# Pace of the projection, four held half tiles, and ordered turns in a hybrid attention layer on one core

## The chip, the core and the metric

The kernel runs on one core of a Trainium2 chip. The core has five engines that run their own instruction queues in order: TensorE (PE in the profile, with its weight loads as PEld), VectorE (DVE), ScalarE (ACT), GpSimd (POOL) and SyncE (SP, which issues the DMAs here). The metric is device microseconds of one launch. The time before is the median of three runs, 1719.52 us (1718.66 to 1720.41).

## What is computed

One layer of a streaming encoder over 1024 prompt tokens, and over 8 x 16 new tokens with caches of 1024 past frames. Everything is float32.

```python
h = rmsnorm(x, g_mix)
q_a, k_a, v_a, q_b, k_b, v_b = split_heads(h, w_in)      # group A: 8 heads x 64, group B: 8 heads x 64
a = stick_breaking(q_a, k_a, v_a)                        # causal over the full past, no softmax
o_b = chunk_band_prompt(q_b, k_b, v_b, rel_table)        # own chunk of 64 and the 8 before, with a bias
a, o_b = per_head_rmsnorm(a), per_head_rmsnorm(o_b)
x = x + concat(a, o_b) @ w_out
h = rmsnorm(x, g_ffn)
x = x + (silu(h @ w_gate) * (h @ w_up)) @ w_down
x = x + sigmoid(rmsnorm(x, g_ple) @ w_ple_gate) * (p @ w_ple_proj)
y = rmsnorm(x, g_final)
```

Stick-breaking: with z the scaled scores, the weight of key k for query q is sigmoid(z) times the product of sigmoid(-z) over the keys between them. The new tokens do the same against their caches, and the new keys and values are outputs too.

## The kernel before

**Number format and tiles.** Each float32 operand of a large product is split into a high part (a cast on ACT, L159) and a low part (a subtraction, `sub`, L105, on POOL or DVE), and `mm3` (L99 to L102) issues three matmuls for each product. Tokens come in nine tiles of 128: 0 to 7 are the prompt, 8 holds the new tokens.

**Order of the work.** Python generators yield after a step, and `advance(main, side, ratio)` (L733) runs `ratio` steps of `side` for each step of `main`. This gives the program order. Outside the blocks that order an engine by hand, a planner then walks the program with a model of the engines' times: on each engine it issues the earliest instruction in program order that its model holds to be ready, so a later instruction can be pulled ahead of an earlier one that still waits. The order that comes out is fixed, and each engine's queue then keeps it on the chip. `tc.issue_after(ins)` ties the instructions of its block that run on the engine of `ins` behind `ins`; those on other engines stay free. The tie is an order and no semaphore.

**Stages around the change.**

- The q/k/v projection (`qkv`, L227) yields 96 steps. Its last 30 (`others` for the values of group B, `queries` of group B) run beside the attention: `advance(project, att, 1.95)` at L818.
- The attention (`attention`, L515) goes through eight pairs of heads, 0 to 3 of group A and 4 to 7 of group B, and through 8 query tiles of each head: 128 units. A step does `scores` of unit i (S, L579 and L580), `flip` of unit i-5 (transposes of the weights, L610, a cast on ACT, L614, and a subtraction on DVE), and `outputs` of two units at a time (`po`, L633 and L634). In group A, `scores` has two sigmoids on ACT (L582, L583), the running product as two scans on DVE (L111 over the tile's own 128 keys, L114 over the keys before) and a product on POOL (L592); in group B, a bias and a minimum on DVE (L586) and an exponential on ACT (L594). When both heads of a pair are done, `turn` (transposes L648, reductions L649 and L654) and `finish` (power and products on POOL, L121 and L671) write the pair's normed output to DRAM (`mixp`); the last pair stays in SBUF (`osb`).
- When the projection has ended, its pools are closed and the decode of group B (`decode`, L334) begins, with `embed` (L827), in the same places. Three attention steps go before and 40 beside them (L875, L877).
- Then the output projection's upper half (`half_out`, L925): the heads of pairs 0 to 3 are loaded (`fetch_mix`, L888, tile `mixn`, four buffers), turned (`turn_mix`, L901: three transposes on PE, L904, a scaled copy on ACT, L907, a subtraction on DVE, L908) and multiplied with the upper 512 rows of `w_out`: 18 half tiles, one for each token tile and each half of the 1024 columns, 12 matmuls of 512 columns each. x is added on DVE (L937) and the sum goes to DRAM (`resid`). One of these steps goes beside each attention step (L947), then come the turns of pairs 4 to 6 and, after the attention, of pair 7 (L950).
- `w_b` (L952) are the lower 512 rows of `w_out`. Weights have one raw buffer and two pairs of places for their parts; L952 takes the places of the two halves before it in turn.
- The next stage (from L1096) adds the lower half for each token tile (`lower`, L996, tile `ps`), in the order 0, 4, 1, 5, 2, 6, 8, 3, 7, with the second column half two tiles behind the first, and goes on to the norm and the feed-forward part.

PSUM has two banks for turns and half tiles (tag M), which both use.

Of the kernel before, what the change touches and what calls it, by code (L numbers as in the profile page):

```python
# [13 lines left out]
F32 = mybir.dt.float32  # L14
# [3 lines left out]
ALU = mybir.AluOpType  # L18
# [4 lines left out]
P = 128  # L23
# [3 lines left out]
NT = 9  # L27
# [5 lines left out]
SKEW = 2  # L33
R2 = 1.2
LAG, RAWS, PT = 5, 7, 2
VLAG, AHEAD = (2, 1), 2


@with_exitstack
def tile_hymba_step(  # L40
# [37 lines left out]
    nc = tc.nc  # L78
    V, A, G, T = nc.vector, nc.scalar, nc.gpsimd, nc.tensor
# [4 lines left out]
    ident = cst.tile([P, P], F32, name="ident")  # L84
# [7 lines left out]
    x_tok = [x_prompt[0, t * P : (t + 1) * P, :] for t in range(NP)] + [x_sample.rearrange("b i d -> (b i) d")]  # L92
# [6 lines left out]
    def mm3(out, ah, al, bh, bl, start, stop):  # L99
        T.matmul(out, lhsT=ah, rhs=bh, start=start, stop=False)  # L100
        T.matmul(out, lhsT=ah, rhs=bl, start=False, stop=False)  # L101
        T.matmul(out, lhsT=al, rhs=bh, start=False, stop=stop)  # L102
# [113 lines left out]
    resid = dram.tile([NT * P, D], F32, name="resid")  # L216
# [293 lines left out]
            yield  # L510


    kept = []

    def attention(ap_, ps, lag):  # L515
        def prepare(p8):
# [80 lines left out]
        def flip(st, hh, t, w):  # L597
            grp = st["grp"]
            g = t // 2
            kb0 = max(0, t - 4) if grp else 0  # L600
            base = max(0, 2 * g - 4) if grp else 0
            if t % 2 == 0:
                st["wt"] = [ap_.tile([P, 6 + g % 2 * 2, 256], F32R, name=f"wt{n}", tag=f"wta{n}{g % 2}") for n in "hl"]
            wth, wtl = st["wt"]
            nb = t + 1 - kb0
            for c0 in range(0, nb, 4):
                c1 = min(c0 + 4, nb)
                pt = ps["t"].tile([P, 512], F32, name="pt", tag="T")
                for c in range(c0, c1):
                    T.transpose(pt[:, (c - c0) * P : (c - c0 + 1) * P], w[:, c * P : (c + 1) * P], ident)  # L610
                pv = pt[:, : (c1 - c0) * P].rearrange("p (k n) -> p k n", n=P)
                ks = slice(kb0 + c0 - base, kb0 + c1 - base)
                qs = slice((t % 2) * P, (t % 2) * P + P)
                A.copy(wth[:, ks, qs], pv)  # L614
                sub(V, wtl[:, ks, qs], pv, wth[:, ks, qs])
            return st["wt"]

        def outputs(st, hh, g, wt):
            wth, wtl = wt
            grp = st["grp"]  # L620
            base = max(0, 2 * g - 4) if grp else 0
            nkb = 2 * g + 2 - base
            po = ps["t"].tile([P, 512], F32, name="po", tag="T")
            order = [2 * g] + [kb for kb in range(base, 2 * g + 2) if kb != 2 * g]
            for i, kb in enumerate(order):
                c0, c1 = 0, 256
                if kb == 2 * g + 1:
                    c0 = P
                if grp and kb == 2 * g - 4:
                    c1 = P  # L630
                vs = st[hh]["v"][:, kb].rearrange("p a d -> p (a d)")
                dst = po[:, c0:c1]
                T.matmul(dst, lhsT=vs, rhs=wth[:, kb - base, c0:c1], start=(i == 0), stop=False)  # L633
                T.matmul(dst, lhsT=vs, rhs=wtl[:, kb - base, c0:c1], start=False, stop=(i == nkb - 1))  # L634
            if g == 0:
                st["ob"] = ap_.tile([P, D], F32, name="ob", tag="ob", bufs=1)
            A.copy(st["ob"][:, g * 256 : g * 256 + 256], po[:, :256])
# [81 lines left out]
    ps = {}  # L719
# [13 lines left out]
    def advance(main, side, ratio, steps=None):  # L733

        due, n = 0.0, 0
        while steps is None or n < steps:
            if next(main, "end") == "end":
                break
            n += 1
            due += ratio  # L740
            while due >= 1.0:
                due -= 1.0
                next(side, None)
        return n

    ch = Chunks(pool(ctx, "w1", "left"), "w", 2048, 1, 2)
    hp = pool(right, "h1", "right")
    stg = pool(right, "stg", "right", 2)
    first, start = ExitStack(), ExitStack()
    banks(right, "right", o=2)  # L750
    banks(start, "left", t=4, g=1)
    hT = Transposed()
# [4 lines left out]
    with tc.tile_pool(name="x1", bufs=2, side="right") as xp, tc.manual_schedule(engines=all_engines):  # L757

        xs = []
# [26 lines left out]
        project = qkv(ch, hT, stg, w_first, ch.raw(cols(w_in[0], 3), KT, 256))  # L786
# [28 lines left out]
    at = pool(left, "at", "left")  # L815
    run, pairs, done = attention(at, ps, LAG)
    att = run(range(8))
    advance(project, att, 1.95)  # L818
    right.close()


# [37 lines left out]
    def chain(*parts):  # L859
        for p_ in parts:  # L860
            yield from p_
# [19 lines left out]
    hT = Transposed()  # L881
# [3 lines left out]
    mp = pool(dstack, "mp", "right", 2)  # L885
# [15 lines left out]
    def turn_mix(k, g, srcs):  # L901
        pt = ps["m"].tile([P, 384], F32, name="pt", tag="M")
        for o, src in enumerate(srcs):
            T.transpose(pt[:, o * P : (o + 1) * P], src, ident)  # L904
        h, l = hT.rows(g, k)
        gk = g_out[:, k : k + 1]
        A.activation(h, pt, AF.Copy, scale=gk)  # L907
        V.scalar_tensor_tensor(l, pt, gk, h.bitcast(F32), op0=ALU.mult, op1=ALU.subtract)  # L908

    def mix(ks):  # L910

        got = []
        for k in ks:
            while k not in done:
                yield
            for g in range(3):
                got.append((k, g, fetch_mix(k, g)))
                if len(got) > 2:
                    turn_mix(*got.pop(0))
                yield  # L920
        for x in got:
            turn_mix(*x)
            yield

    def half_out():  # L925

        yield from mix(range(4))
        for c in range(2):
            wh, wl = out_weights(0, c)
            for t in range(NT):  # L930
                cs = slice(c * 512, (c + 1) * 512)
                xs = mp.tile([P, 512], F32, name="xs", tag="xs", bufs=3)
                nc.sync.dma_start(xs, x_tok[t][:, cs])
                acc = ps["m"].tile([P, 512], F32, name="acc", tag="M")
                for k in range(4):
                    mm3(acc, *hT.tok(t, k), wh[:, k], wl[:, k], k == 0, k == 3)
                V.tensor_tensor(xs, xs, acc, op=ALU.add)  # L937
                nc.sync.dma_start(resid[t * P : (t + 1) * P, cs], xs)
                yield

    def out_weights(grp, c):

        return ch.load(w_out[0, grp * 512 : grp * 512 + 512, c * 512 : (c + 1) * 512].rearrange("(k p) c -> p k c", p=P),
                       4, 512)

    side = chain(half_out(), mix(range(4, 7)))
    advance(att, side, 1.0)  # L947
    for _ in side:
        pass
    for _ in mix([7]):  # L950
        pass
    w_b = [out_weights(1, c) for c in range(2)]  # L952
    left.close()
    dstack.close()
    hstack[0].close()
# [135 lines left out]
    marks = []  # L1091

    A.activation(xg.tile([P, 1], F32, name="any", tag="r_n"), nhalf[:, 0:1], AF.Sigmoid)
    order = [0, 4, 1, 5, 2, 6, 8, 3, 7]
    xs, first_half, rows = {}, {}, []
    fetch(order[0], 0)  # L1096
    with ExitStack() as planned:
        for i in range(NT + SKEW):
# [14 lines left out]
            if j == NT - 2:  # L1113
                w = gate_up_parts(raw, V)
# [15 lines left out]
    with tc.tile_pool(name="ph4b", bufs=2, side="right", reuse_waits="tile") as p4b:  # L1130
# [12 lines left out]
        for i in range(n_chunk):  # L1143
# [25 lines left out]
            c = bank()  # L1169
# [546 lines left out]
```

## Time and profile before

| | us |
|---|---|
| median of three timed runs | 1719.52 |
| the profiled execution, in all | 1712.64 |
| its span, first to last instruction | 1710.6 |

The profile is of that one execution. A row of a stage gives its stretch, its length, the busy time of each engine with the number of instructions, the mean granted TensorE clock (1.00 is full speed), the busy share of the DMA engines and the data rate. A row of a group names line, engine and operation, what is written from what, the count, then the busy time and the mean ns of one, and the idle time before them with what ended it. A row of a wait names who waited for whom, with the sum in us, the number of times and the longest. A row of the timeline starts with the start in us and the duration; in brackets is the idle time of the engine before it. Matmuls overlap in the pipeline, so their rows' durations add to more than the time that they take; the distance from start to start is what one costs in a row of them.

### The profile page before, as it was taken

How to read it: one execution, taken by the hardware profiler on the slowest of the kernel's cores; microseconds unless marked ns; L12 is line 12 of the kernel's file. 1: busy time of each engine (PE TensorE's matmuls, PEld its weight loads, DVE VectorE, ACT ScalarE, POOL GpSimd, SP SyncE). 2: the span in 40 equal slices, each digit the busy share in tenths (PEclk: the TensorE clock that was granted, in tenths of full speed). 3: DMA queues.
4: the chain of work that ended last, by engine and by line, in shares of the span. 5: the costliest groups of instructions: out<-in, count | busy, mean ns of one | idle time of the engine just before them, and what ended most of it. 6: DMA issues, size and time to landing. Idle time of an engine off the chain costs nothing.

```text
span 1710.6 us, 27738 instructions
## 1 busy us (share of the span) xinstructions
PE 1651.7 (97%) x10308; PEld 1421.3 (83%) x10308; DVE 1099.0 (64%) x1716; ACT 807.1 (47%) x1713; POOL 805.7 (47%) x652
## 2 busy tenths in 40 slices
PE   8999999989997999898989999999999999999998
PEld 7999888989996887787868888888888878878887
DVE  6111444379889666854787666666565597798875
ACT  5323545366778777643543233333332244433673
POOL 2313301277356411322345555555555379968763
PEclk9999999999998999999999999999999999999999
DMA  5847888665369885854422222222222597722222
GB/s 193 276 151 219 275 292 293 187 187 168 116 181 277 276 266 163 252 176 169 153 82 96 96 96 95 96 93 87 86 89 95 214 367 256 257 79 111 99 98 99
DMA packets 172810, 293.49 MB, mean 172 GB/s; under 512 B 16642, under 2 KB 96258, under 8 KB 170371
## 3 DMA queue, kind: packets, MB, share of 16 engines
q1 hardware_dynamic: 172674, 291.71, 52.0%
q8 instruction: 82, 1.34, 0.3%
q14 instruction: 54, 0.43, 0.1%
HBM read 204.77 MB, written 86.90 MB: 171 GB/s over the span
## 4 chain that ended last, share of the span: by engine, by line
PE 78%; DVE 7%; DMA 6%; ACT 3%; POOL 3%; issue 2%; SPq 1%; POOLq 0%; DVEq 0%; ACTq 0%
PE ps L1058 24%; PE ps L100 6%; PE ps L101 6%; PE ps L102 6%; PE pt L1321 4%; PE pt L1058 3%; PE ps L1321 3%; PE pt L610 2%; PE pt L405 2%; PE acc L468 2%; DMA v<-sv 2%; DVE keep L114 2%; PE po L634 1%; PE sdec L427 1%; PE S L579 1%
## 5 line engine op out<-in xcount | busy, mean ns | idle before, releaser
L105 POOL TENSOR_TENSOR wlo<-wraw,whi 128x512 fp32r<-128x512 f32 (+1 forms) x119 | 211.3, 1798 | 139.7 <-ACT whi L159 138.5
L100 PE MATMUL ps<-whi,hTh 128*128 128x256 f32 x576 | 167.7, 291 | 1.3 <-ACT st L267 1.3
L101 PE MATMUL ps<-wlo,hTh 128*128 128x256 f32 x576 | 164.2, 285 | 0.0
L102 PE MATMUL ps<-whi,hTl 128*128 128x256 f32 x576 | 163.7, 284 | 0.1
L159 ACT CAST whi<-wraw 128x512 fp32r<-128x512 f32 (+1 forms) x122 | 88.6, 744 | 71.4 <-PE ps L1058 28.6
L100 PEld LDWEIGHTS ps<-whi,hTh 128*128 128x128 f32 x576 | 110.4, 192 | 7.9 <-issue 5.7
L592 POOL TENSOR_TENSOR w<-w,keep 128x127 f32<-128x127 f32 (+4 forms) x64 | 78.6, 1230 | 74.8 <-DVE keep L114 64.5
L102 PEld LDWEIGHTS ps<-whi,hTl 128*128 128x128 f32 x576 | 110.4, 192 | 0.8 <-DVE hTl L105 0.4
L101 PEld LDWEIGHTS ps<-wlo,hTh 128*128 128x128 f32 x576 | 110.5, 192 | 0.2
L614 ACT CAST wth<-pt 128x512 fp32r<-128x512 f32 (+1 forms) x192 | 84.4, 466 | 44.5 <-PE pt L610 43.9
L105 DVE TENSOR_TENSOR wtl<-pt,wth 128x512 fp32r<-128x512 f32 (+1 forms) x192 | 94.1, 513 | 14.8 <-ACT wth L614 14.7
L114 DVE TENSOR_TENSOR_SCAN keep<-keep,zero 128x128 f32<-128x128 f32 (+7 forms) x64 | 101.6, 1588 | 1.7
L610 PE MATMUL pt<-ident,w 128*128 128x128 f32 x528 | 90.4, 284 | 8.5 <-DVE wtl L105 4.4
L610 PEld LDWEIGHTS pt<-ident,w 128*128 128x128 f32 x528 | 64.2, 144 | 21.6 <-DVE wtl L105 6.0
L579 PE MATMUL S<-qk 128*128 128x384 f32 (+2 forms) x192 | 71.9, 376 | 6.5 <-ACT keep L583 4.4
L633 PE MATMUL po<-wth,vk 128*128 128x256 f32 (+1 forms) x304 | 76.5, 283 | 1.5 <-DVE wtl L105 1.2
L105 POOL TENSOR_TENSOR actl<-actr,acth 128x1024 fp32r<-128x1024 f32 (+1 forms) x22 | 61.2, 2782 | 34.2 <-DMA sr<-acts 20.7
L634 PE MATMUL po<-wtl,vk 128*128 128x256 f32 (+1 forms) x304 | 73.4, 285 | 0.0
L406 DVE COPY kT<-pt 128x512 f32<-128x512 f32 x48 | 33.0, 687 | 53.4 <-PE pt L405 49.5
L101 PE MATMUL ps<-hTl,whi 128*128 128x384 f32 x192 | 65.4, 341 | 0.0
L102 PE MATMUL ps<-hTh,wlo 128*128 128x384 f32 x192 | 65.3, 340 | 0.0
L100 PE MATMUL ps<-hTh,whi 128*128 128x384 f32 x192 | 65.3, 340 | 0.0
(441 smaller groups left out, 5292.1 us busy)
## 6 DMA issues: line engine op xcount, KB each, us to landing
draw<-in_cache_sb_k SPq DMA_DIRECT2D x32, 512.0 KB, 5.7
draw<-in_cache_sb_v SPq DMA_DIRECT2D x32, 512.0 KB, 5.7
act<-sg SPq DMA_DIRECT2D x11, 1152.0 KB
actr<-act SPq DMA_DIRECT2D x22, 576.0 KB, 9.5
wraw<-in_w_in SPq DMA_DIRECT2D x11, 1024.0 KB, 8.7
wraw<-in_w_gate SPq DMA_DIRECT2D x11, 1024.0 KB, 5.5
wraw<-in_w_up SPq DMA_DIRECT2D x11, 1024.0 KB, 5.4
v<-sv SPq DMA_DIRECT2D x36, 256.0 KB, 4.7
```

Of the source, the lines that this page charges most:

```text
L100: T.matmul(out, lhsT=ah, rhs=bh, start=start, stop=False)
L101: T.matmul(out, lhsT=ah, rhs=bl, start=False, stop=False)
L102: T.matmul(out, lhsT=al, rhs=bh, start=False, stop=stop)
L105: return eng.tensor_tensor(out, a, hi.bitcast(F32), op=ALU.subtract)
L114: V.tensor_tensor_scan(rev, rev, zero[:, 0:1].to_broadcast([P, n - d]), keep[:, n - d : n - d + 1], op0=ALU.mult, op1=ALU.max)
L159: A.copy(h[:, o], v[:, o])
L579: T.matmul(sc, lhsT=hd["qq"][:, qs], rhs=hd["kkh"][:, kc], start=True, stop=False)
L610: T.transpose(pt[:, (c - c0) * P : (c - c0 + 1) * P], w[:, c * P : (c + 1) * P], ident)
L614: A.copy(wth[:, ks, qs], pv)
L634: T.matmul(dst, lhsT=vs, rhs=wtl[:, kb - base, c0:c1], start=False, stop=(i == nkb - 1))
L1058: T.matmul(out, lhsT=a[x][:, k], rhs=b[y][:, k], start=(not more and k == 0 and n == 0), stop=(k == 3 and n == 2), skip_group_check=more)
L1321: T.matmul(out, lhsT=a[i][:, x, m * P : (m + 1) * P], rhs=b[j][:, x], start=(not more and x == 0 and n == 0), stop=(x == 1 and n == 2), sk ...
```

## The change

The pace of the attention beside the projection goes from 1.95 to 2.13 steps. `flipped` keeps the last transpose or output matmul that the attention has traced, and all turns of pairs 0 to 6 that run beside or right behind the attention are tied behind it on PE. The half tiles take the order of the next stage; the last four of the second column half (token tiles 6, 8, 3, 7) are taken out of the steps beside the attention and traced after the turns of pairs 4 to 6, tied behind the attention's last output matmul. The second of the two lower weight halves gets its low part from DVE instead of POOL.

```diff
+HELD = 4
+ORDER = [0, 4, 1, 5, 2, 6, 8, 3, 7]
...
-    kept = []
+    kept, flipped = [], []
...
-                    T.transpose(pt[:, (c - c0) * P : (c - c0 + 1) * P], w[:, c * P : (c + 1) * P], ident)
+                    flipped[:] = [T.transpose(pt[:, (c - c0) * P : (c - c0 + 1) * P], w[:, c * P : (c + 1) * P], ident)]
...
-                T.matmul(dst, lhsT=vs, rhs=wtl[:, kb - base, c0:c1], start=False, stop=(i == nkb - 1))
+                flipped[:] = [T.matmul(dst, lhsT=vs, rhs=wtl[:, kb - base, c0:c1], start=False, stop=(i == nkb - 1))]
...
-    advance(project, att, 1.95)
+    advance(project, att, 2.13)
...
                 if len(got) > 2:
-                    turn_mix(*got.pop(0))
+                    with tc.issue_after(flipped[0].ins):
+                        turn_mix(*got.pop(0))
                 yield
         for x in got:
-            turn_mix(*x)
+            with tc.issue_after(flipped[0].ins):
+                turn_mix(*x)
             yield
+
+    def half_tile(t, c, wh, wl):
+        cs = slice(c * 512, (c + 1) * 512)
+        xs = mp.tile([P, 512], F32, name="xs", tag="xs", bufs=3)
+        nc.sync.dma_start(xs, x_tok[t][:, cs])
+        acc = ps["m"].tile([P, 512], F32, name="acc", tag="M")
+        for k in range(4):
+            mm3(acc, *hT.tok(t, k), wh[:, k], wl[:, k], k == 0, k == 3)
+        V.tensor_tensor(xs, xs, acc, op=ALU.add)
+        nc.sync.dma_start(resid[t * P : (t + 1) * P, cs], xs)
 
     def half_out():
 
         yield from mix(range(4))
         for c in range(2):
             wh, wl = out_weights(0, c)
-            for t in range(NT):
...
+            for t in ORDER if c == 0 else ORDER[:-HELD]:
+                half_tile(t, c, wh, wl)
                 yield
+        held.append((wh, wl))
...
+    def out_weights(grp, c, eng=None):
+
+        src = w_out[0, grp * 512 : grp * 512 + 512, c * 512 : (c + 1) * 512].rearrange("(k p) c -> p k c", p=P)
+        return ch.parts(ch.raw(src, 4, 512), 4, 512, 2, eng)
+
+    held = []
     side = chain(half_out(), mix(range(4, 7)))
     advance(att, side, 1.0)
     for _ in side:
         pass
+    with tc.issue_after(flipped[0].ins):
+        for t in ORDER[-HELD:]:
+            half_tile(t, 1, *held[0])
     for _ in mix([7]):
         pass
-    w_b = [out_weights(1, c) for c in range(2)]
+    w_b = [out_weights(1, c, (None, V)[c]) for c in range(2)]
```

The body that `half_tile` takes over is that of the loop before; only its place is new. `order` of the next stage becomes the same `ORDER`.

More of the change, by code (lines that the diff above doesn't have):

```diff
@@ L929, in half_out @@
             wh, wl = out_weights(0, c)
-            for t in range(NT):
[L931 to L938, printed above, removed]
-                yield
-    def out_weights(grp, c):
-        return ch.load(w_out[0, grp * 512 : grp * 512 + 512, c * 512 : (c + 1) * 512].rearrange("(k p) c -> p k c", p=P),
-                       4, 512)
+            for t in ORDER if c == 0 else ORDER[:-HELD]:
+                half_tile(t, c, wh, wl)
+                yield
+        held.append((wh, wl))
[3 more added lines that the diff above has]
+    held = []
     side = chain(half_out(), mix(range(4, 7)))
@@ L1093, in tile_hymba_step @@
     A.activation(xg.tile([P, 1], F32, name="any", tag="r_n"), nhalf[:, 0:1], AF.Sigmoid)
-    order = [0, 4, 1, 5, 2, 6, 8, 3, 7]
+    order = ORDER
     xs, first_half, rows = {}, {}, []
```

## The prediction

> **What bounds the kernel now.** I read the page first, for the busy shares, the chain that ended last and its own span.
>
> ```profile
> span 1710.6 us, 27738 instructions
> PE 1651.7 (97%) x10308; PEld 1421.3 (83%) x10308; DVE 1099.0 (64%) x1716; ACT 807.1 (47%) x1713; POOL 805.7 (47%) x652
> PE 78%; DVE 7%; DMA 6%; ACT 3%; POOL 3%; issue 2%; SPq 1%; POOLq 0%; DVEq 0%; ACTq 0%
> ```
>
> TensorE (PE) is the bound: 97% busy, 78% of the chain. The change adds no matmul and removes none, so the only time to win is time in which PE waits or runs at a lower granted clock. Next I cut the attention part at its seams, found in the timeline: 508.5 is the last projection matmul, 683.7 the first load of finished heads, 717.7 the first matmul of the half output projection (`acc`), 793.5 the attention's last output matmul (`po`), 814.2 the moment from which matmuls run without a break again.
>
> ```profile
> core 0: us, PE busy (x) PEld busy (x) DVE busy (x) ACT busy (x) POOL busy (x), PEclk, DMA share, GB/s
> 332.40:508.50 176.10, 169.28 (x1215) 162.86 (x1216) 145.09 (x199) 120.40 (x297) 103.20 (x131) 1.00 0.59 171
> 400.00:508.50 108.50, 106.94 (x734) 103.80 (x733) 96.31 (x134) 76.85 (x183) 58.34 (x74) 1.00 0.53 154
> 508.50:560.50 52.00, 42.81 (x304) 34.91 (x303) 47.01 (x72) 40.14 (x97) 32.64 (x41) 0.84 0.86 249
> 560.50:683.70 123.20, 121.21 (x1094) 99.54 (x1093) 82.32 (x264) 90.32 (x246) 34.10 (x43) 1.00 0.79 240
> 683.70:717.70 34.00, 27.27 (x190) 24.84 (x189) 28.69 (x83) 24.96 (x67) 11.69 (x11) 0.90 0.92 262
> 717.70:793.50 75.80, 75.80 (x433) 65.58 (x432) 39.62 (x102) 30.53 (x74) 14.47 (x10) 1.00 0.52 173
> 793.50:814.20 20.70, 15.73 (x82) 11.84 (x81) 8.99 (x17) 8.70 (x16) 7.52 (x5) 0.92 0.53 177
> ```
>
> The reader should see three holes, and each is where the change works. I count a hole as idle time plus busy time times the missing clock. **Tail of group A** (508.5 to 560.5): 9.2 idle + 0.16 x 42.8 = 6.8, together 16.0 us. **Turn stage** (683.7 to 717.7): 6.7 + 0.10 x 27.3 = 9.5 us. **End** (793.5 to 814.2): 5.0 + 0.08 x 15.7 = 6.2 us. Between them PE is full. What PE waits for, by the view of waits, stage by stage:
>
> ```profile
> PE pt L610 <- DVE wtl L105: 2.5, 3, 1.7
> PE sdec L427 <- ACT keep L583: 1.6, 1, 1.6
> PE po L633 <- DVE wtl L105: 1.2, 1, 1.2
> ...
> PE pt L904 <- DMA mixn<-mixp: 5.4, 2, 3.2
> PE pt L610 <- ACT w L594: 0.8, 1, 0.8
> ...
> PE pt L904 <- DMA mixn<-mixp: 3.9, 1, 3.9
> PE pt L904 <- DVE hUl L908: 0.8, 2, 0.5
> ```
>
> First block: in the tail PE waits for VectorE (DVE) and for the sigmoids behind it; DVE is busy 47.0 of 52.0 there. Second and third block: in the turn stage and at the end PE stands behind a turn (L904) whose heads have not landed.
>
> **Part 1, the pace 1.95 to 2.13.** The projection has 30 steps left here, so 58 attention steps (30 x 1.95) become 63 (30 x 2.13) of the 64 units of group A: five more units go beside projection matmuls. The scans of L111, one for each unit, count them:
>
> ```profile
> L111 DVE TENSOR_TENSOR_SCAN keep<-keep,ident 128x128 f32<-128x128 f32 x33 | 21.8, 663 | 8.8 <-ACT keep L583 8.8
> ...
> L111 DVE TENSOR_TENSOR_SCAN keep<-keep,ident 128x128 f32<-128x128 f32 x12 | 8.2, 686 | 1.2 <-ACT keep L583 1.2
> L406 DVE COPY kT<-pt 128x512 f32<-128x512 f32 x5 | 3.4, 674 | 0.7 <-PE pt L405 0.7
> ```
>
> 33 units in 400 to 508.5 (3.3 us each, PE full) and 12 in the tail (4.3 us each). So the projection ends in the queue 12 units before the last scan, not five, as the planner pulls its matmuls forward. If the shift of five carries over, 5/12 of the tail's 16.0 us go: 6.7. The other bound is 0, if DVE cannot take the five beside the projection: about 40 us of its 47.0 are group A's (the rest is decode work such as L406), 3.3 a unit, 16.7 for five. Its free time over 332.4 to 508.5 is 176.1 - 145.1 = 31.0, so on average they fit, though 8.8 of the free time in the second half is waiting for `keep` from ACT. I take **4.5**, two thirds of the full gain, since the row with room is the nearer one. What is late next: the decode of group B, which starts where the projection's pools close, moves back by up to 5 x 4.3 = 21.7 us of the old tail. Its PE work is conserved and lands in 560.5 to 683.7, where PE is 121.2 of 123.2 busy at full clock. Its DMAs move too (third rival).
>
> A sentence on a rule: the Trainium skill, "TensorE: Matmul & The Clock Gate", section "HAM oscillation — how this bites in real kernels", lets the clock fall only behind PE gaps of more than about 3.4 us. The trace disagrees in the tail: its longest wait is 1.7 us in the rows above, and yet
>
> ```profile
> 520.00:530.00 10.00, 5.97 (x25) 4.42 (x24) 9.93 (x13) 4.97 (x13) 8.46 (x8) 0.63 1.09 312
> 806.00:810.00 4.00, 3.86 (x14) 2.99 (x15) 1.24 (x2) 1.16 (x2) 0.00 (x0) 0.59 0.04 12
> ```
>
> 0.63 was granted in 520 to 530. By the rule the tail would hold 9.2 us of loss, its term would be 2.6 and the sum 8 instead of 10; the measured clock decides. Behind the 3.9 us wait of the end (second row) rule and row agree.
>
> **Part 2, turns in program order.** Twelve turns (three for each of four pairs) lie in the turn stage. The order binds PE alone: a turn may not pass the flip or output traced last before it. Nothing on ACT, DVE or SP is held.
>
> ```profile
> 683.71 1.41 SPq L894 DMA_DIRECT2D mixn<-mixp  x3
> 688.61 0.55 PE L904 MATMUL pt<-ident,mixn 128*128 128x128 f32 x3 [2.18 <-DMA mixn<-mixp]
> ...
> L610 PE MATMUL pt<-ident,w 128*128 128x128 f32 x54 | 9.8, 303 | 0.9 <-ACT w L594 0.8
> ...
> L100 PE MATMUL acc<-whi,hUh 128*128 128x512 f32 x72 | 29.7, 412 | 0.0
> L633 PE MATMUL po<-wth,vk 128*128 128x256 f32 (+1 forms) x48 | 11.4, 270 | 0.0
> ```
>
> Today the planner puts the first turn close behind its load, ahead of attention work, and PE waits 2.2 and later 3.2 us. Held behind the flips, a turn comes later and its heads have landed. The upper bound is what DVE, the busiest engine here, leaves: 34.0 - 28.7 = 5.3. The lower: 54 flips at five a unit are 11 units in 34 us, 3.1 each; in program order the turns take 14 steps, so up to three more would pass before the first half tile can fill PE. A unit alone keeps PE busy 1.6 us (last two rows, 717.7 to 793.5: 72/4 = 18 tiles of 2.8 us leave 26 of the 75.8 for 48 outputs, six for two units, 16 units). That is 3 x 1.5 = 4.5 lost. I take a gain of **1**, a little above the middle, since both waits on record are for DMAs that a later turn finds landed.
>
> **Part 3, four half tiles held.** One is 12 matmuls of 512 columns:
>
> ```profile
> 775.37 0.40 PE L101 MATMUL acc<-wlo,hUh 128*128 128x512 f32 x1
> 775.60 0.39 PE L102 MATMUL acc<-whi,hUl 128*128 128x512 f32 x1
> ...
> 793.41 0.28 PE L634 MATMUL po<-wtl,vk 128*128 128x128 f32 x1
> ...
> 798.84 2.90 POOL L121 TENSOR_TENSOR r_o<-r_o,nhalf 128x16 f32<-128x16 f32 x1 [2.97 <-DVE r_o L120]
> 802.13 2.04 POOL L671 TENSOR_TENSOR osb<-osb,r_o 128x512 f32<-128x512 f32 x2
> ...
> 806.11 1.51 PE L904 MATMUL pt<-ident,mixn 128*128 128x128 f32 x6 [3.87 <-DMA mixn<-mixp]
> ```
>
> 0.23 us from start to start, 2.8 a tile, 11.0 for four. They leave 717.7 to 793.5, where PE stays full: steps without a half tile at the end go from four to three (31 attention steps against 14 + 14 steps of turns and tiles, before 36 against 14 + 18). They come back behind the last `po`. The last pair's chain from there to its scaled heads is 793.4 to 804.2, 10.8 us, just the length of four tiles. So the whole hole of 6.2 can go. It need not: the order is planned, and if the turn at 806.11 is again placed where its heads ought to have landed but have not, its 3.9 us and the cold clock's 1.3 stay, and 1.0 is won. I take **4.5**. The tiles' loads and stores are the same four pairs of DMAs, later on SP, and their four sums on DVE likewise. The resid rows of tiles 6, 8, 3, 7 are read back only at the end of the next stage, in the same order.
>
> The price is `w_b[1]`: its buffer is free only behind the last held tile. Then ACT casts and DVE subtracts.
>
> ```profile
> L105 DVE TENSOR_TENSOR wlo<-wraw,whi x13: 682/1226/3005, 10.4 to 1613.2; 128x1024 fp32r<-128x1024 f32 x8, 128x512 fp32r<-128x512 f32 x5
> 790.72 2.40 POOL L105 TENSOR_TENSOR wlo<-wraw,whi 128x1024 fp32r<-128x1024 f32 x1 [31.46 <-ACT whi L159]
> 792.38 1.05 ACT L159 CAST whi<-wraw 128x1024 fp32r<-128x1024 f32 x1 [0.60 <-PE acc L102]
> ```
>
> 1.05 + 1.23 = 2.3 us behind the last tile, against 3.5 with POOL. `lower` starts with three tiles of the other half (8.3 us), which hide it; without that cover it costs 2.3. The load of the first gate weights waits for the same single raw buffer, some 15 us later than now, and is used only beside the last tile but one of the next stage. The tile order of the first half is free: the same units, with all their heads turned.
>
> **The sum.** 4.5 + 1 + 4.5 = 10 us. The profiled execution took 1712.64 in all (span 1710.6), the median of the three timed runs is 1719.52; I take the 10 off the median: **1709.5** (span 1700.6 by the same step). Full gains would be 6.7 + 5.3 + 6.2 = 18.2, 1701.3; the lower ends make 0 - 4.5 + 1.0 = 3.5 slower, 1723.
>
> **The rivals.** *The tail stays.* The planner pulled the projection 12 units ahead and may do so again; then DVE bounds the same units alone, and only parts 2 and 3 give: 5.5, **1714**. For it: DVE 47.0 of 52.0. Against: the new program order gives the units earlier, and 31.0 us of DVE lie free.
>
> *The waits come back.* All three holes are re-planned, and the turns again stand before their DMAs, the tail before DVE: **1719**, near the lower ends of parts 1 and 3 with nothing from part 2. For it: both `mixn` waits come from loads that land later than the order reckons with, and the change does not touch the loads. That is also the case in which the change does not do what it says.
>
> *The group B loads collide* (slower). The decode's caches are
>
> ```profile
> L141 SPq DMA_DIRECT2D draw<-in_cache_cb_k x16: 368/385/532, 504.2 to 622.0; - x16
> L141 SPq DMA_DIRECT2D draw<-in_cache_cb_v x16: 368/382/924, 512.4 to 637.0; - x16
> ```
>
> 32 loads of 512 KB, 16.8 MB in 133 us, 126 GB/s beside the attention's own. A start 21.7 us later pushes 2.7 MB into a stretch that already moves 240 GB/s, 29.6 MB in 123.2 us. If 240 is what the queue yields there, that is 11 us more, against at most 6.7 won in the tail, and `mixn` waits (9.3 us in all) grow by a fifth: 4.3 + 1.9 = 6 slower, **1725.5**. It decides where the stage needs over 262 GB/s and does not get it. Against it: 312 GB/s stands in the row for 520 to 530, and no wait of PE for a DMA leads the list in 560.5 to 683.7.
>
> **How the numbers follow.** The forecast gets 0.47, the staying tail 0.20, no change 0.18, the collision 0.15. 0.2% of 1719.5 is 3.4 us, about what a measurement of this kernel can tell from no change. Forecast and staying tail are faster by more, less a slice of 0.01 that falls short: faster 0.66, same 0.19, slower 0.15. The range goes from 1700, just past the full gains, to 1723, the sum of the lower ends; it leaves most of the collision out.
>
> **What would show it.** Part 1: the projection's last matmul stands about seven scans before the last one, the stretch behind it is near 30 us, its clock above 0.84. Part 2: no L904 wait over 1 us beside attention. Part 3: four half tiles behind the last `po`, no PE wait of several us up to the steady `lower` matmuls. Wrong would be: a `mixn` wait of 3 us still there, DVE near 100% before the projection ends, or PE waiting for `kT` or DMA in the decode.

## The result and the profile after

| | us, median | range | runs |
|---|---|---|---|
| before | 1716.73 | 1712.94 to 1720.41 | 21 |
| changed | 1720.25 | 1715.66 to 1723.47 | 21 |

The ratio is 1.0021, with a 95% interval from 1.0013 to 1.0029: about 3.5 us slower, where 10 us faster was forecast. Both medians come from the same sessions; a second, unchanged copy of the kernel before came out at 0.9994 (0.9981 to 1.0006) against it, so 0.1% is about what two sets of runs differ by anyway.

The profiled execution, 1723.47 us in all, is the longest of its range, that of before (1712.64) lies just below the range above. The span is 10.5 us longer, and 4.2 of these lie ahead of the first attention score (332.4 against 336.6), where nothing was changed. So single traces are compared here by stretches and holes, and totals by the timed runs. The head of the page, of the changed kernel:

```profile
span 1721.1 us, 27743 instructions
PE 1657.1 (96%) x10308; PEld 1422.9 (83%) x10308; DVE 1096.6 (64%) x1718; ACT 803.5 (47%) x1711; POOL 802.4 (47%) x650
```

TensorE is still the bound, with the same 10308 matmuls. The stages of the changed kernel, cut at the same events as before (columns as in the prediction's table of stages), and its scans behind the projection's last matmul:

```profile
336.60:513.40 176.80, 169.99 (x1216) 164.01 (x1217) 144.96 (x199) 120.71 (x297) 103.21 (x131) 0.99 0.59 170
513.40:566.00 52.60, 41.91 (x273) 34.17 (x272) 48.50 (x73) 38.57 (x98) 37.60 (x42) 0.87 0.79 227
566.00:703.10 137.10, 134.14 (x1187) 107.00 (x1186) 91.94 (x302) 98.27 (x270) 38.91 (x49) 1.00 0.78 235
703.10:738.80 35.70, 30.11 (x225) 27.50 (x225) 28.18 (x85) 27.26 (x73) 5.94 (x7) 0.95 0.90 260
738.80:791.50 52.70, 52.70 (x289) 45.19 (x287) 23.33 (x57) 15.76 (x38) 9.94 (x6) 1.00 0.46 148
791.50:825.00 33.50, 26.05 (x127) 20.70 (x127) 13.92 (x23) 10.86 (x18) 5.17 (x4) 0.95 0.51 154
```

```profile
L113 DVE TENSOR_TENSOR_SCAN keep<-keep,ident 128x128 f32<-128x128 f32 x12 | 9.0, 753 | 1.8 <-ACT keep L585 1.8
```

With the same measure of a hole (idle time plus busy time times the missing clock):

| hole, us | before | changed |
|---|---|---|
| tail of group A | 16.0 | 10.7 + 5.4 = 16.1 |
| decode stage | 2.0 | 3.0 |
| turn stage | 9.5 | 5.6 + 1.5 = 7.1 |
| end | 6.2 | 7.45 + 1.3 = 8.8 |

The tail is what it was: the projection ends 176.8 us after the first score (before 176.1), and twelve scans, not seven, stand behind it. The decode stage is 14 us longer and the half-tile stage 23 us shorter: five units moved from one to the other, and the four held tiles (11 us) went to the end. The end's hole grew.

These holes grow by 1.3 us together, from 33.7 to 35.0, while the stretch from the first score to the first transpose of the next norm is 7.0 us longer. Here it is as a whole in before, in the changed kernel, and in two kernels of the experiments below, e1 (the pace alone) and e10 (the changed kernel with a shorter decode stage):

```profile
332.40:822.70 490.30, 460.60 (x3344) 406.51 (x3345) 356.54 (x743) 318.34 (x798) 205.45 (x242) 0.97 0.67 203
336.60:833.90 497.30, 463.79 (x3344) 405.85 (x3345) 356.29 (x745) 314.80 (x796) 202.61 (x240) 0.98 0.67 200
333.50:827.70 494.20, 465.08 (x3345) 406.19 (x3344) 354.33 (x743) 315.18 (x796) 207.32 (x242) 0.98 0.68 201
332.30:822.10 489.80, 460.06 (x3344) 405.17 (x3345) 358.54 (x745) 315.42 (x796) 202.35 (x240) 0.98 0.69 203
```

Busy time times clock is PE's work at full clock: 447 us in before, 454 in the changed kernel, 456 with the pace alone, 451 in e10, for the same number of matmuls but for one. In six traces at pace 1.95 (before, e2, e3, e6, e9, e12) it is 447 to 449, in five at 2.13 (the changed kernel, e1, e4, e5, e11) 452 to 456; the rounding of the clock alone is worth 2 us. So with the new pace PE works about 5 us longer on the same matmuls. That is no hole, and the table above leaves it out. Which matmuls take longer, and why, stays open.

What PE does at the end, in the changed kernel's timeline, and ACT beside it:

```profile
801.04 0.87 PE L906 MATMUL pt<-ident,mixn 128*128 128x128 f32 x3 [4.58 <-DMA mixn<-mixp]
...
819.30 0.39 PE L104 MATMUL acc<-whi,hUl 128*128 128x512 f32 x1
819.53 0.49 PE L906 MATMUL pt<-ident,osb 128*128 128x128 f32 x3
822.86 0.49 PE L102 MATMUL ps<-whi,hUh 128*128 128x512 f32 x1 [2.85 <-ACT hUh L909]
```

```profile
818.41 1.05 ACT L161 CAST whi<-wraw 128x1024 fp32r<-128x1024 f32 x1 [9.70 <-PE acc L104]
819.78 1.04 ACT L161 CAST whi<-wraw 128x1024 fp32r<-128x1024 f32 x1 [0.32 <-PE acc L104]
820.85 1.28 ACT L1105 ACT_TABLE_LOAD   x1
...
822.25 0.56 ACT L909 ACTIVATE hUh<-pt,g_out 128x384 fp32r<-128x384 f32 x1
```

The held tiles do lie behind the last output, but not in the hole. PE first stands 4.58 us at a turn of pairs 4 to 6 whose heads have not landed; the tiles come only behind these turns and end at 819.7. Then the last pair's first turn runs, and PE waits another 2.85 us, because in ACT's queue its scaled copy (822.25) stands behind the casts of the second lower weight half and the next stage's table load. The casts wait for the last held tile.

### The profile page after: what moved, and what is told of

Its sections match the earlier page's. It is cut to its first block, busy times and chain, and to the rows that moved or that the text cites. A ratio compares the mean times of both kernels' runs of the same rounds, so it can differ in the third digit from the quotient of the medians.

```text
span 1721.1 us, 27743 instructions
## 1 busy us (share of the span) xinstructions
PE 1657.1 (96%) x10308; PEld 1422.9 (83%) x10308; DVE 1096.6 (64%) x1718; ACT 803.5 (47%) x1711; POOL 802.4 (47%) x650
## 4 chain that ended last, share of the span: by engine, by line
PE 80%; DVE 7%; DMA 5%; ACT 3%; POOL 2%; issue 2%; SPq 0%; POOLq 0%; DVEq 0%; ACTq 0%
PE ps L1070 24%; PE ps L102 7%; PE ps L103 6%; PE ps L104 6%; PE pt L1333 5%; PE ps L1333 4%; PE pt L1070 3%; PE pt L407 2%; PE pt L612 2%; PE acc L470 2%; DVE keep L116 2%; DMA v<-sv 2%; PE sdec L429 2%; PE po L636 1%; PE S L581 1%
## 5 line engine op out<-in xcount | busy, mean ns | idle before, releaser
L107 POOL TENSOR_TENSOR wlo<-wraw,whi 128x512 fp32r<-128x512 f32 (+1 forms) x117 | 206.0, 1785 | 119.6 <-ACT whi L161 119.6
```

The lines of the kernel that those rows point to most:

```text
L107: return eng.tensor_tensor(out, a, hi.bitcast(F32), op=ALU.subtract)
```

## The experiments

**My theory ahead of them** was that the pace did nothing for the tail and the loss was made at the end, by the order there. Rivals: the later decode costs the time (B), or the ties do (C). All ratios are against the kernel before, from 11 or 12 runs of each kernel (21 of the changed one, 5 of e7):

| run | what is in it | ratio | 95% interval |
|---|---|---|---|
| changed | pace 2.13, ties, held tiles | 1.0021 | 1.0013 to 1.0029 |
| e1 | pace 2.13 | 1.0004 | 0.9994 to 1.0014 |
| e2 | ties | 1.0014 | 1.0004 to 1.0024 |
| e3 | held tiles | 0.9983 | 0.9974 to 0.9992 |
| e4 | changed, held tiles ahead of the turns | 1.0022 | 1.0012 to 1.0031 |
| e5 | pace 2.13, held tiles | 1.0016 | 1.0003 to 1.0029 |
| e6 | held tiles, last pair's copies first on ACT | 0.9974 | 0.9963 to 0.9986 |
| e7 | pace 2.13, projection tied to the attention | 1.0109 | 1.0095 to 1.0123 |
| e8 | pace 1.75, held tiles | 1.0016 | 1.0007 to 1.0025 |
| e9 | ties, held tiles | 0.9982 | 0.9970 to 0.9993 |
| e10 | changed, decode beside 35 steps | 0.9994 | 0.9982 to 1.0005 |
| e11 | changed, last pair's copies first on ACT | 1.0013 | 0.9998 to 1.0027 |
| e12 | the kernel before again | 0.9994 | 0.9981 to 1.0006 |

"Held tiles" includes their tile order and DVE for the last low part.

### One part at a time (e1, e2, e3)

```diff
-    advance(project, att, 1.95)
+    advance(project, att, 2.13)
```

> The kernel before with the pace 2.13 and nothing else. Theory A (the loss is made at the end, the pace moves decode work only from the tail into the stage behind it): within 2 us of the kernel before; twelve scans still behind the projection's last matmul, tail hole about 16 us as before. Rival B (the five units that the decode starts later cost time): 3 to 5 us slower than before, with more idle or slower clock between 560 and 700. The prediction on record would have it 4.5 us faster.

Measured 0.04%: nothing. The time is as theory A has it and B's 3 to 5 us are not there, though PE's work is 5 us or more above that of before, as shown above; smaller holes make up for it. The scans behind its projection:

```profile
L111 DVE TENSOR_TENSOR_SCAN keep<-keep,ident 128x128 f32<-128x128 f32 x12 | 9.0, 751 | 1.8 <-ACT keep L583 1.8
```

One thing in its trace I had not expected: with the pace alone, and no tile held, four half tiles already lie behind the last output. Its timeline:

```profile
788.27 0.28 PE L634 MATMUL po<-wtl,vk 128*128 128x128 f32 x1
...
800.07 0.39 PE L102 MATMUL acc<-whi,hUl 128*128 128x512 f32 x1
```

They come ahead of the turns there. The stretch from the last output to the first transpose of the next norm, by the view of windows, has a hole of 3.6 + 0.04 x 35.8 = 5.1 us:

```profile
788.30:827.70 39.40, 35.76 (x167) 28.08 (x166) 16.45 (x30) 14.14 (x25) 11.66 (x8) 0.96 0.61 198
```

e2 keeps only the ties: the changed kernel at pace 1.95, with

```diff
-            for t in ORDER if c == 0 else ORDER[:-HELD]:
+            for t in range(NT):
...
-    with tc.issue_after(flipped[0].ins):
-        for t in ORDER[-HELD:]:
-            half_tile(t, 1, *held[0])
...
-    w_b = [out_weights(1, c, (None, V)[c]) for c in range(2)]
+    w_b = [out_weights(1, c) for c in range(2)]
```

> The changed kernel with the old pace, without held tiles, without the new tile order and with POOL for the low part of the lower weights: only the ties on the turns are left. Theory A: 0 to 3 us faster than before (turn-stage hole 9.5 falls to about 7), the wait for the heads of the last pairs behind the last output stays near 4 us. Rival C (the ties hold turns too late, and half tiles start later): 2 to 5 us slower than before.

Measured 0.14% slower, 2.4 us: theory A missed, C came in. The wait for the heads in its turn stage is no shorter than before (5.4 us there):

```profile
PE pt L906 <- DMA mixn<-mixp: 6.4, 3, 3.5
```

But the unchanged kernel's second trace (e12) has 6.6 us in the same row, so this is no cause, and which step costs the 2.4 us stays open; beside held tiles the ties cost nothing (e9 against e3, below).

e3 keeps only the held tiles: the changed kernel at pace 1.95, with `turn_mix` taken out of its two ties.

```diff
-                    with tc.issue_after(flipped[0].ins):
-                        turn_mix(*got.pop(0))
+                    turn_mix(*got.pop(0))
...
-            with tc.issue_after(flipped[0].ins):
-                turn_mix(*x)
+            turn_mix(*x)
```

> The changed kernel with the old pace and without the ties on the turns: held tiles, tile order, and the low part on DVE. Theory A: 2 to 4 us slower than before if the held tiles again stand behind turns whose heads have not landed (a wait of over 3 us behind the last output, ahead of the first held tile) and the last pair's turn again stands behind the casts of the lower weights; faster by 3 to 5 if without the ties the planner puts the tiles first. Rivals B and C: same as before or faster, as the loss would lie in the part left out.

Measured 0.17% **faster**, 2.9 us. The three parts add up to 0.01%, and the changed kernel stands at 0.21%. Each part's interval is 0.1% wide to either side, so the sum alone proves little. I took it that no part carries the loss and two of them spoil each other; the pairs below bear that out.

### Which two (e5, e9, e10)

What I now looked for is what differs at the end. The transposes of turns behind the last output, by the view of groups, in before, in the changed kernel and in e3, two rows each:

```profile
L904 PE MATMUL pt<-ident,mixn 128*128 128x128 f32 x28 | 5.3, 307 | 4.4 <-DMA mixn<-mixp 3.9 <-DVE hUl L908 0.5
L904 PE MATMUL pt<-ident,osb 128*128 128x128 f32 x8 | 1.4, 279 | 0.3 <-DVE hUl L908 0.3
```

```profile
L906 PE MATMUL pt<-ident,mixn 128*128 128x128 f32 x28 | 5.4, 305 | 4.6 <-DMA mixn<-mixp 4.6
L906 PE MATMUL pt<-ident,osb 128*128 128x128 f32 x8 | 1.2, 272 | 0.0
```

```profile
L906 PE MATMUL pt<-ident,mixn 128*128 128x128 f32 x13 | 2.1, 284 | 0.0
L906 PE MATMUL pt<-ident,osb 128*128 128x128 f32 x8 | 1.8, 364 | 0.0
```

28 + 8 transposes are twelve turns: all of pairs 4 to 6 and the last pair. 13 + 8 are seven. Four tiles held give four more steps beside the attention to turns (**theory D**); five units moved to the decode take them back. The steps count it: the half stage has 36 attention steps at pace 1.95 and 31 at 2.13; to be run beside them are 14 steps of the first turns, 18 tiles and 11 steps of the last three pairs' turns. Before, 43 - 36 = 7 steps are left over; with held tiles 39 - 36 = 3; in the changed kernel 39 - 31 = 8.

e5 takes the ties out of the changed kernel (the edit of e3, at pace 2.13).

> The changed kernel without the ties on the turns (pace 2.13, held tiles, DVE for the last low part stay). Theory D (the pace takes five steps from the stage in which half tiles and turns run beside the attention, so the turns of the last pairs fall behind its last output, with or without ties, and the held tiles behind them): the wait of over 4 us behind the last output and the 2.85 us wait of the last pair stay; 0 to 2 us faster than the changed kernel, still 1.5 us or more slower than the kernel with held tiles alone. Rival C (the ties are what undoes the held tiles): the 4.6 us wait goes, and the time falls to within 1.5 us of the kernel with held tiles alone, 5 to 6 us below the changed kernel.

Measured 1.0016: 0.05% below the changed kernel, 0.33% above e3, and both waits are there. Rival C falls. Its waits behind the last output:

```profile
PE pt L906 <- DMA mixn<-mixp: 3.8, 1, 3.8
PE ps L102 <- ACT hUh L909: 2.8, 1, 2.8
```

e9 puts back the pace alone.

```diff
-    advance(project, att, 2.13)
+    advance(project, att, 1.95)
```

> The changed kernel with the old pace 1.95 (ties, held tiles and DVE's low part stay). Theory D (the new pace takes five steps from the stage with the half tiles; with held tiles and the old pace eight of eleven turn steps of the last three pairs still lie beside the attention, with the new pace three): 3 to 5 us faster than the changed kernel, within 2 us of the kernel before, since the ties cost about what the held tiles give. Rival C (the ties undo the held tiles at any pace): within 1.5 us of the changed kernel.

Measured 0.9982, 0.39% or 6.7 us below the changed kernel, a little more than expected, and 3.1 us below the kernel before, where within 2 was expected. The turns behind its last output and its waits there:

```profile
L906 PE MATMUL pt<-ident,mixn 128*128 128x128 f32 x19 | 3.1, 275 | 0.3 <-DVE hUl L910 0.3
L906 PE MATMUL pt<-ident,osb 128*128 128x128 f32 x8 | 1.2, 272 | 0.0
```

```profile
PE ps L102 <- ACT hUh L909: 2.8, 1, 2.8
```

Nine turns instead of twelve, and the wait for the heads is gone. By the steps, six of the nine turns of pairs 4 to 6 should have gone beside the attention; three did (five in e3). So the count of steps tells the direction, not the exact number.

e10 leaves the pace at 2.13 and gives the half stage its five steps back from the decode.

```diff
-    advance(att, beside, 1.0, 40)
+    advance(att, beside, 1.14, 35)
```

> The changed kernel, with the decode of group B spread over 35 instead of 40 attention steps (1.14 decode steps beside each), so that the stage with the half tiles has its five attention steps back although the pace is 2.13. Theory D: 3 to 5 us faster than the changed kernel, the wait of 4.6 us behind the last output under 2 us. Rival I (the new pace is paid for in the decode stage, where the matmuls took 3 us more, by the later decode itself): within 1.5 us of the changed kernel, wherever the end stands.

Measured 0.9994, 0.27% or 4.6 us below the changed kernel, with the end of e9 (19 + 8 transposes, no wait for heads). So with held tiles the new pace need not lose the time, if the half stage gets its steps back. Rival I as it was put falls. But e10 does two things, as the five steps also leave the decode stage: in the traces its holes over the whole stretch are 38.9 us against the changed kernel's 42.8, and PE's work is 451 against 454. No run gives the half stage its steps and leaves the decode as it is, so how much of the 4.6 us each of the two is worth isn't shown. Whether the 0.12% between e10 and e9 is real, the intervals don't tell.

The stretch from the last output to the first transpose of the next norm, in the changed kernel, e9 and e10, by the view of windows:

```profile
791.40:833.90 42.50, 35.05 (x168) 28.08 (x167) 19.38 (x33) 14.22 (x25) 7.00 (x6) 0.96 0.60 195
```

```profile
792.80:827.40 34.60, 31.51 (x156) 25.93 (x155) 17.23 (x30) 12.39 (x22) 7.01 (x6) 1.00 0.56 191
```

```profile
787.50:822.10 34.60, 31.51 (x156) 25.88 (x155) 17.17 (x30) 12.39 (x22) 7.01 (x6) 1.00 0.54 191
```

The changed kernel takes 42.5 us for it, with a hole of 7.45 + 0.04 x 35.05 = 8.9. In e9 and e10 the hole is 34.6 - 31.5 = 3.1, 5.8 us less. The number of turns left is not all of it: e1, with the same twelve turns and four tiles behind its last output, has 5.1, and before, with twelve turns, 6.4. The 8.9 belong to twelve turns with the tiles behind them.

### The order at the end (e4, e6, e11)

e4 is the changed kernel with the held tiles traced ahead of the turns that are left.

```diff
     advance(att, side, 1.0)
-    for _ in side:
-        pass
     with tc.issue_after(flipped[0].ins):
         for t in ORDER[-HELD:]:
             half_tile(t, 1, *held[0])
+    for _ in side:
+        pass
```

> The changed kernel, only the held tiles are traced straight behind the attention, ahead of the turns of pairs 4 to 6 that are left. Theory A: the wait of 4.6 us behind the last output and the slow clock behind it go, 4 to 6 us faster than the changed kernel, 1 to 3 faster than before; the 2.85 us wait for the last pair's scaled heads may stay. Rivals B and C: under 1 us faster than the changed kernel.

Measured 1.0022: no gain. The wait went where it was expected to, and the time did not follow. Its waits behind the last output, and the stretch:

```profile
PE ps L102 <- ACT hUh L909: 3.8, 4, 2.8
PE pt L906 <- DMA mixn<-mixp: 0.8, 1, 0.8
```

```profile
788.70:830.20 41.50, 36.90 (x168) 28.95 (x168) 19.31 (x32) 13.83 (x25) 7.27 (x6) 0.92 0.60 194
```

3.8 of the 4.6 us are won, but the waits for ACT grow by 1.0 and the clock falls to 0.92, which costs 36.9 x 0.08 = 3.0 us (1.4 in the changed kernel). The stretch is 1.0 us shorter, and the timed runs show nothing of it. My first theory, that the place of the tiles among the turns is the loss, falls with it, as a change of place alone wins nothing here. e1 has the same order with a hole of 5.1 against 7.6 here; which of the other edits makes that difference is not shown.

e6 is e3 with the casts of the second lower weight half and the next stage's first activation tied on ACT behind the last pair's copies.

```diff
+    copied = []
...
-        A.activation(h, pt, AF.Copy, scale=gk)
+        copied[:] = [A.activation(h, pt, AF.Copy, scale=gk)]
...
-    w_b = [out_weights(1, c, (None, V)[c]) for c in range(2)]
+    w_b = [out_weights(1, 0)]
+    with tc.issue_after(copied[0].ins):
+        w_b.append(out_weights(1, 1, V))
...
-    A.activation(xg.tile([P, 1], F32, name="any", tag="r_n"), nhalf[:, 0:1], AF.Sigmoid)
+    with tc.issue_after(copied[0].ins):
+        A.activation(xg.tile([P, 1], F32, name="any", tag="r_n"), nhalf[:, 0:1], AF.Sigmoid)
```

> The kernel with held tiles alone (pace 1.95, no ties on the turns), and on ACT the casts of the second lower weight half and the activation of the next stage tied behind the last pair's scaled copies. Theory E (the last pair's heads wait for ACT, which stands behind those casts): the 2.8 us wait behind the last pair's first turn goes and the clock stays full, 2 to 4 us faster than the kernel with held tiles alone. Rival F (the casts are then late for the lower matmuls of the second column half, and PE waits there as long): no gain, a wait of 2 us or more for the weights after it.

Measured 0.9974, the best of all and below both kernels, though only 0.09% (1.6 us) below e3, where theory E had 2 to 4 us, and inside what the intervals leave open. PE's waits behind its last output:

```profile
PE ps L103 <- DVE wlo L107: 1.0, 1, 1.0
PE pt L908 <- DVE xs L936: 0.5, 1, 0.5
PE ps L102 <- ACT whi L161: 0.5, 1, 0.5
```

The last pair's copies now come ahead of the casts. The 2.8 us wait is gone, and 2.0 us of smaller ones stand in its place, two of them for the weights: rival F is half right. But the clock over the stretch is 1.00 (0.95 in e3), and its hole 1.9 us (4.4 in e3). e11 does the same to the changed kernel.

> The changed kernel, with the casts of the second lower weight half and the next stage's activation tied on ACT behind the last pair's scaled copies. Theory E: the 2.85 us wait goes, 1.5 to 3 us faster than the changed kernel, the 4.6 us wait for the heads stays. Rival F: no gain, as PE waits for the weights instead.

Measured 1.0013, 0.08% below the changed kernel, not to be told from nothing. The last pair's wait for ACT is gone. The wait for the heads (first row) is 2.8 us here, and PE waits 2.0 us for the weights (second row):

```profile
PE pt L908 <- DMA mixn<-mixp: 2.8, 1, 2.8
PE ps L103 <- DVE wlo L107: 2.0, 1, 2.0
```

So that wait was worth less than its length: the weights behind it are late as well. The clock over the stretch is 0.92 (0.96 in the changed kernel), and its hole stays at 8.7.

### What a moved projection would be worth (e7, e8)

e7 does what the pace was meant to do, on the kernel before: each projection step is tied on PE behind the attention's last flip or output, which `flipped` keeps as in the change.

```diff
...
-    advance(project, att, 1.95)
+    due = 0.0
+    while True:
+        with (tc.issue_after(flipped[0].ins) if flipped else ExitStack()):
+            if next(project, "end") == "end":
+                break
+        due += 2.13
+        while due >= 1.0:
+            due -= 1.0
+            next(att, None)
```

> The kernel before with pace 2.13, and every projection step tied on PE behind the attention's last flip or output ahead of it in program order, so that the planner can no longer pull the projection forward; turns and half tiles as before. Theory G (the prediction's first term was right for a projection that really is dealt out): the projection ends six or seven scans before the last scan instead of twelve, the tail hole falls from 16 to 8 to 11 us, and the time is 3 to 7 us below the kernel with pace 2.13 alone. Rival H (PE then waits for VectorE beside the projection): the tail hole falls, but as much idle time appears before the projection's end; within 2 us of the kernel with pace 2.13 alone.

Measured 1.0109, 18.7 us slower: G falls, and H was too kind. The projection now ends three scans ahead of the last one, and the tail is gone. The view of windows has it up to the projection's end, in the tail, and in the decode stage; below stand PE's longest waits up to the projection's end:

```profile
331.90:547.80 215.90, 198.21 (x1392) 188.00 (x1393) 167.60 (x235) 136.78 (x342) 121.06 (x155) 0.97 0.54 153
547.80:563.80 16.00, 13.62 (x103) 11.99 (x102) 13.34 (x21) 12.75 (x30) 6.71 (x9) 1.00 0.94 291
563.80:719.70 155.90, 142.22 (x1235) 114.11 (x1234) 96.86 (x318) 108.08 (x292) 48.97 (x59) 0.96 0.80 236
```

```profile
PE po L633 <- DVE wtl L105: 8.9, 4, 6.0
PE S L579 <- DMA qk<-kT0h: 5.7, 1, 5.7
```

The hole in the tail is 2.4 us instead of 16, but 23.6 stand ahead of it (8.8 in e1, in 177 us) and 19.4 behind it (2.9 in e1, from 564.0 to 701.0). PE waits for single things there, for a low part of the weights up to 6.0 us and for keys from DRAM 5.7, while DVE is busy only 168 of 216 us: the tie leaves PE no projection matmul to take meanwhile. The tie and the pace are the only edits here and the pace alone cost nothing, so it was the planner's pulling forward that had hidden these waits.

e8 turns the pace the other way, on e3.

```diff
-    advance(project, att, 1.95)
+    advance(project, att, 1.75)
```

> The kernel with held tiles alone at pace 1.75 (52 instead of 58 units of attention in program order beside the projection): the pace the other way. Theory D: the projection's end does not move against the first score (within 1 us), twelve scans stay behind it, the decode starts earlier in the tail and PE spends 3 us less on the stretch up to the first turns, but the attention's last units then stand alone at the end without half tiles: between 3 us faster and 3 us slower than the kernel with held tiles alone. The prediction's first term, turned round, would have it 4 to 6 us slower, with some 18 scans behind the projection.

Measured 1.0016, 0.33% or 5.7 us above e3, outside theory D's range. The projection ended 173.1 us after the first score, 3 us earlier than in before, with fourteen scans behind it: the pace does move it, by two units for six. Its tail and its end, by the view of windows:

```profile
505.20:582.40 77.20, 62.18 (x485) 48.08 (x484) 57.86 (x101) 59.70 (x136) 44.22 (x53) 0.91 0.87 256
796.20:825.80 29.60, 29.26 (x138) 23.95 (x136) 13.48 (x23) 9.13 (x16) 7.00 (x6) 1.00 0.56 195
```

Here only the last pair's three turns are left behind the last output and the end's hole is 0.3 us, as theory D has it, but the tail, now 77 us long, has one of 15.0 + 5.6 = 20.6. PE's work over the whole stretch, by the measure above, is 454 us here too (447 in e3), so the tail's hole is not all that this pace costs. With tiles held, both neighbours of 1.95 lose 0.3%.

### How far two sets of one kernel differ (e12)

> The kernel before, unchanged, against itself: how far two sets of runs and two traces of one kernel lie apart. Within 0.1% of before; first score between 332 and 337 us, the sum of PE's waits between first score and first norm transpose 27 to 31 us.

Measured 0.9994. In its trace PE's waits between first score and first norm transpose are 29.6 us (29.2 in the one shown), the tail hole 16.0, the end hole 5.5 (6.4 over the same stretch), but the turn stage's is 11.8 against 9.5:

```profile
685.10:722.30 37.20, 29.48 (x198) 27.06 (x197) 29.82 (x87) 26.17 (x69) 12.36 (x12) 0.86 0.86 246
```

So 2 us of that hole are chance, and the 7.1 of the changed kernel is little proof of a gain there.

## Why the prediction was wrong, step by step

**Part 1 (4.5).** The step that failed is "If the shift of five carries over, 5/12 of the tail's 16.0 us go". It did not carry over: twelve scans, 16.1 us of hole in the changed kernel, and 0.04% for the pace by itself. The planner pulled the projection forward as before, as the rival of the staying tail had it. The argument behind it, that 31 us of free DVE time make room for the five units, fell too: where the projection really moved (e7), DVE had its room, and PE stood for the delay of single results. Free time on average is not a result in time. "What is late next" named only the decode; that the five units were missing from the half stage went unpriced. A second step failed there: "Its PE work is conserved". The matmuls are the same, but PE worked about 5 us longer on them in the five kernels with the new pace and the old decode stage (452 to 456 against 447 to 449). So "the only time to win is time in which PE waits or runs at a lower granted clock" left out a term, and a loss of that size was in no sum.

**Part 2 (1, bounds -4.5 to 5.3).** Inside its bounds, on the wrong side: 2.4 us slower alone, about nothing beside held tiles. "Its heads have landed" is not what the trace shows: the turn stage still holds 4.3 us of waits for `mixn` in the changed kernel, 6.4 in e2.

**Part 3 (4.5, bounds 1.0 to 6.2).** The mechanism was right, and held tiles alone gave 2.9 us. In the changed kernel they gave nothing (e5 stands 0.12% above e1, the same pace without them), and the step that failed is the count "31 attention steps against 14 + 14 steps of turns and tiles, before 36 against 14 + 18". It left out the eleven steps of the last pairs' turns, which use the same attention steps and come last. With them it reads 31 against 39, before 36 against 43: the held tiles make room for four steps and the pace takes five. The count gives the direction only: before and the changed kernel both end with twelve turns. The bound of the case that the turn is again placed ahead of its heads was written down and thought the less likely one. The price of `w_b[1]` was looked for on `lower` and hidden there; it fell on the last pair's copy, behind it in ACT's queue, 2.85 us.

**The rivals.** The staying tail was right for part 1, the returning waits for part 3; the colliding loads were not seen: the `mixn` waits of the turn stage did not grow (4.3 against 5.4), and the decode stage's hole rose by only 1.0 us. PE's longer work on the same matmuls was in none of them. The time lies 1.25 us above the 1719 of the returning waits, inside the range, but against a median of before that had come down by 2.8 us with more runs, and so on the other side.

The parts were summed as if each had its own room. Two of them lived on the same five steps.

## What to carry to other kernels

When two edits of an interleaved program both move work across the same boundary, count everything that shares the slots there, the work that comes last above all, before their gains are added; then measure each alone and the pairs. A pace written in program order says little of where a reordering planner puts a matmul: count in the trace what stands behind the seam. And a wait that is taken away is worth its length only if nothing that follows it is late as well. Last, add up the holes and compare the sum with the stretch: what is missing is time in which the bound engine works longer on the same instructions.

## What the runs showed of the hardware

The clock fell behind a pause that no single wait makes long. In e1, PE did 1.1 us of work in 3.41, with waits of 0.45 and 1.85 us between short turns, and the next 3.41 us ran at 0.50:

```profile
800.59:804.00 3.41, 1.11 (x7) 0.61 (x5) 0.98 (x2) 3.38 (x5) 3.41 (x4) 1.00 0.89 220
804.00:807.41 3.41, 3.41 (x11) 2.66 (x10) 0.76 (x2) 0.52 (x2) 2.35 (x2) 0.50 0.97 352
```

In the changed kernel the same 0.50, for the same 3.41 us, follows the 4.58 us wait, of which the first row shows a part:

```profile
797.14:800.55 3.41, 0.00 (x0) 0.00 (x0) 0.36 (x1) 0.00 (x0) 3.25 (x3) 1.00 0.89 254
800.55:803.96 3.41, 2.92 (x11) 2.45 (x11) 0.62 (x1) 0.58 (x1) 1.37 (x2) 0.50 0.83 255
```

So in e1 a sparse stretch cost what a pause more than twice as long as its longest wait did. In the fourteen traces, up to the last 20 us of the span, the clock fell 89 times, always to 0.50 and for 3.41 us or two or three times that, and each time PE had been busy at most 2.15 us of the 3.41 just ahead. The rule that the prediction weighed, from the Trainium skill, "TensorE: Matmul & The Clock Gate", section "HAM oscillation — how this bites in real kernels", asks for no idle gaps of PE over about 3.4 us; the fall in the changed kernel agrees with it, the one in e1 came without such a gap.
